# Moving two triangular systems and the sums of W_down inside an encoder layer on one core

## The chip, the core and the metric

The kernel runs as one program on 1 core of a Trainium2 chip. The metric is the device time of one execution in microseconds (us). A core has five engines: TensorE (PE; its weight loads are listed apart as PEld), VectorE (DVE), ScalarE (ACT), GpSimd (POOL) and SyncE (SP). SP computes nothing here; its queue issues most of the DMAs, in the order of the queue. Large weights are loaded through ACT's queue from the RWKV part on.

## What is computed

One layer (DEPTH = 1) over 1024 tokens of width 1024, all in float32:

```python
h = rmsnorm(x, g_mix[i])
z = h @ w_in[i]                       # FoX q, k, v, f | RWKV r, k, v, dw, da, dg | two gates
...
y_fox = fox_attention(q, k, v, log_f) # 8 heads of 64, causal, blocks of 128 queries
...
yr = rwkv7_scan(rh, decay, kh, vh, -kk, kk * ah)   # 8 heads of 64, a delta rule
y_rwkv = (yr + bonus) * g
merged = gate_fox * (y_fox @ w_o_fox[i]) + gate_rwkv * (y_rwkv @ w_o_rwkv[i])
x = x + merged @ w_out[i]
h2 = rmsnorm(x, g_ffn[i])
u = causal_dwconv(h2 @ w_up[i], conv_w[i], conv_b[i])
x = x + (gelu(u[..., :D_FF]) * u[..., D_FF:]) @ w_down[i]
ple_gate = sigmoid(rmsnorm(x, g_ple[i]) @ w_ple_gate[i])
x = x + ple_gate * (p[i] @ w_ple_up[i])
```

## The kernel before

**Arithmetic.** A float32 product is made of three matmuls: each operand is split into a high part (a cast on ACT) and the remainder (a subtraction, `L208`, on DVE), and high times high, low times high and high times low are added up in PSUM (`L236` to `L238` for most projections, `L734` and `L739` to `L741` for those of attention). The wide stage behind attention (FFN, `L1156`, `L1332`) is not touched.

**Stages in the order of the program.** Norm of x and the narrow projections; four calls of `rwkv_pre`, one per pair of RWKV heads (call 1 is `hp = 0`, call 4 is `hp = 3`); `fox_z(0)`, the projection of attention's first head pair, and `forget`, the forget gates; four pairs of attention (`fox_att`), each beside the projection of the next pair; then the RWKV chunk chain, gates, W_out, FFN.

**A call of `rwkv_pre`.** Projection of k (`L236` to `L238`); small products `L361` and `L369`; cumulative decay `L377`; norms of k: PE `L387`, DVE's root, ACT's copy `L394`, PE's transposes `L401`, DVE `L402` (`kkn`); projection of r; DVE `L407` to `L409` (`AR`), `L419` to `L423` (`kkn`, `kr`, `bk`), `L426` (`rk`); projection of v; `L433` (gate); transposes of v, `L442`; `L451` and DVE `L452`; then two groups of eight chunks: scores `L465` on PE, masked by DVE into `sc` (`L468`), stored by SP (`L474` to `L480`), transposes `L485` on PE, copied by ACT into `bt` (`L486`) and stored (`L488` to `L490`). SP also stores `AR` (`L412` to `L414`), the gate (`L435`), the transposed v (`L445`, `L446`) and `bvd` (`L453`).

**A triangular system, `tsolve(hp)`.** It needs the stored `sc` of call `hp + 1`. SP loads `tA` (`L513`, four DMAs), the generator yields `tlag`, POOL makes two copies into `tT` (`L517`), DVE does thirty steps of a product and an addition (`L521`, `L523`) and two memsets (`L527`): 62 DVE instructions in one chain, then SP stores and ACT copies the result (`L529` to `L532`). `tmerge` (`L548` to `L567`) makes the full inverse from it later, on PE.

**A sum of W_down, `down_sums`.** Eleven of them. SP loads two rows of blocks into `wt`, the only buffer (`L1258`), POOL makes four subtractions (`L1260` to `L1263`), SP stores four results (`L1266`), which the FFN reads.

**What sets the order.** Every stage is a generator that yields the cost of what it has issued, and `interleave` takes the generator that has done the least share of its stated cost:

```python
it = min(live, key=lambda e: e[2] / e[1])
it[2] += next(it[0]) or 0.0
```

The framework then orders each engine's instructions anew by its own estimate of when inputs will be there, so an operation can stand far from the place where the text issues it. Within an engine and a queue, that order is kept at run time.

In the kernel before, systems 1 to 3 (`tsolve(0)` to `tsolve(2)`) are beside calls 2 to 4, with `tlag` 30; system 4 (`tsolve(3)`) is beside `fox_z(0)`, with `tlag` 12; gate block 0 (`gate_early(0)`, whose matmuls read `gwh` and `gwl`) is beside call 4, block 1 beside `forget`; the sums are beside attention of pairs 1 to 3; the merges of systems 1 and 2 are beside pair 2, those of 3 and 4 beside pair 3.

Of the kernel before, what the change touches and what calls it, by code (L numbers as in the profile page):

```python
# [12 lines left out]
F32 = mybir.dt.float32  # L13
# [7 lines left out]
P = 128  # L21
# [6 lines left out]
HP = 4  # L28
DFF = 2816
NFB = DFF // P  # L30
# [22 lines left out]
def flat(gens):  # L53
    for g in gens:
        yield from g
# [7 lines left out]
def interleave(*parts):  # L63


    live = [[g, n, 0.0] for g, n in parts]
    while live:
        it = min(live, key=lambda e: e[2] / e[1])
        try:
            it[2] += next(it[0]) or 0.0  # L70
        except StopIteration:
            live.remove(it)


def merge(*gens):

    live = list(gens)
    while live:
        for g in list(live):
            try:  # L80
                yield next(g)
            except StopIteration:
                live.remove(g)


class Net:
# [1350 lines left out]
    def body(self, stop):  # L1437
# [63 lines left out]
        self.early = 7  # L1501
        self.cw = 160.0
        self.lora_w()
        self.p1, close_p1 = self.pool("rw", side="right")
        self.tlag = 30.0
        for hp in range(HP):
            side = [(self.tsolve(hp - 1), 40.0)] if hp else []
            if hp == HP - 1:
                side.append((self.gate_early(0, True, 35.0), 45.4))
            interleave((self.rwkv_pre(hp), 36.2), *side)  # L1510
        close_ps()
        close_ps = self.pools(("zp", 2), ("scp", 2), ("trp", 3), ("pvp", 1))
        close_p1()
        close_p0()
        close_wp()

        self.fwp, close_fwp = self.pool("foxw", side="right")
        self.fp, close_fp = self.pool("fox", side="right")
        self.kl = None
        zV, qk = [], []  # L1520
        self.tlag = 12.0
        self.wt, close_wt = self.pool("wt", side="left")
        self.wd2 = {n: self.tc.dram_tile([NFB // 2, P, 512], F32, name="wd" + n) for n in ("t1", "t2", "t3", "t4")}

        z_tile = lambda: self.zp.tile([P, 512], F32, name="z", tag="z")
        interleave((self.fox_z(0, self.fox_w(0), zV), 31.5), (self.tsolve(HP - 1), 22.0))
        interleave((flat([[3.0], merge(self.forget(), self.fox_qk(zV[0], qk))]), 5.7), (self.gate_early(1), 10.4))
        for hp in range(HP):
            att = self.fox_att(hp, qk, zV[1])
            if hp + 1 < HP:  # L1530
                zV, qk = [], []
                interleave((att, 23.0), (self.fox_z(hp + 1, self.fox_w(hp + 1), zV), 31.5),
                           (self.down_sums(range(hp * 4, min(hp * 4 + 4, NFB // 2))), 12.0),
                           *([(flat([self.tmerge(2 * hp - 2, z_tile), self.tmerge(2 * hp - 1, z_tile)]), 24.0)] if hp else []))
                interleave((merge(self.last, flat([[0.0] * 3, self.fox_qk(zV[0], qk)])), 6.0), (self.gate_early(hp + 2), 10.4))
            else:
                n = HP + 1

                def rest():
                    yield from att  # L1540
                    yield from self.last
                interleave((rest(), 25.0), (flat([self.gate_early(j) for j in range(n, self.early)]),
                                            10.4 * (self.early - n)))
        close_ps()
        close_fp()
        close_fwp()
        close_wt()
        close_gwp()
        close_tp()

# [80 lines left out]
        z_tile = lambda: self.zt.tile([P, T], F32, name="zt", tag="zt")  # L1631
# [182 lines left out]
```

## Time and profile before

| what | value |
|---|---|
| median of 3 runs | 1861.44 us (1861.11 to 1862.19) |
| profiled execution, its own time | 1862.91 us |
| its span in the trace | 1860.8 us |
| its mean granted PE clock | 0.988 of full speed |

The profile is of one execution, and its times are those of that execution. A row of the busy times gives an engine's busy time and its count of instructions. PE's matmuls are pipelined, and their ends are modelled. A row of the waits says which engine and line waited, for the instruction of which engine, how long in all, how many times, and the longest. Idle time of an engine on which nothing depends costs nothing.

### The profile page before, as it was taken

What the parts mean: (1) busy time and instruction counts of PE and PEld (TensorE: products, weight loads), DVE (VectorE), ACT (ScalarE), POOL (GpSimd) and SP (SyncE); (2) the same over time, 40 slices, a digit from 0 to 9 for tenths busy, and PEclk for the clock granted to TensorE, in tenths of its full rate; (3) what the DMA queues carried; (4) which work ended last, traced back from release to release, by engine and by line L of the source; (5) the groups of instructions that cost most, each with busy time, mean ns of one, the idle gap of its engine ahead of it and who ended that gap; (6) DMA issues with size and microseconds to landing.
All of it is one profiled execution on the core that took longest, in us unless ns stands there. A gap on an engine that the chain in (4) does not pass through costs nothing.

```text
span 1860.8 us, 28297 instructions
## 1 busy us (share of the span) xinstructions
PE 1789.9 (96%) x10867; PEld 1481.8 (80%) x10867; DVE 1207.4 (65%) x2382; ACT 783.0 (42%) x1236; POOL 357.9 (19%) x251
## 2 busy tenths in 40 slices
PE   5999998899999999999999999999999999999999
PEld 5876777788989776666778987888888888888898
DVE  7538655766565735545435288999899986566752
ACT  4543342457575622223362144344343444434431
POOL 4321001331000000000013304554545531000000
PEclk9999998899999999999999999999999999999999
DMA  6666548453122255545375123333233328655431
GB/s 200 196 195 193 133 92 220 139 158 97 32 75 55 69 137 125 163 134 142 122 245 161 57 91 85 119 107 103 85 97 118 107 95 317 234 198 176 144 117 46
DMA packets 295085, 250.29 MB, mean 135 GB/s; under 512 B 80200, under 2 KB 235550, under 8 KB 294951
## 3 DMA queue, kind: packets, MB, share of 16 engines
q1 hardware_dynamic: 230071, 220.40, 37.5%
q10 hardware_dynamic: 64880, 28.09, 6.0%
q8 instruction: 86, 1.41, 0.3%
q14 instruction: 48, 0.39, 0.1%
HBM read 171.07 MB, written 77.37 MB: 134 GB/s over the span
## 4 chain that ended last, share of the span: by engine, by line
PE 64%; DVE 3%; ACT 2%; DMA 1%; issue 1%; POOL 0%; ACTq 0%; DVEq 0%; POOLq 0%
PE pu L1156 8%; PE pu L1157 8%; PE pu L1158 8%; PE pu L1334 3%; PE pu L1333 3%; PE pu L1332 3%; PE zt L228 3%; PE zt L227 3%; PE zt L229 3%; PE zt L238 2%; PE zt L236 2%; PE zt L237 2%; PE zt L989 2%; PE zt L988 2%; PE zt L987 2%; PE tr L844 1%
## 5 line engine op out<-in xcount | busy, mean ns | idle before, releaser
L1332 PE MATMUL pu<-op 128*128 128x512 f32 x276 | 107.7, 390 | 0.0
L1334 PE MATMUL pu<-op 128*128 128x512 f32 x276 | 107.4, 389 | 0.0
L1333 PE MATMUL pu<-op 128*128 128x512 f32 x276 | 107.4, 389 | 0.0
L207 ACT CAST wh<-wr 128x1024 fp32r<-128x1024 f32 (+1 forms) x43 | 38.1, 889 | 142.4 <-PE zt L237 104.7
L236 PE MATMUL zt<-hah,wh 128*128 128x512 f32 (+1 forms) x200 | 79.4, 398 | 0.0
L237 PE MATMUL zt<-hbl,wh 128*128 128x512 f32 (+1 forms) x200 | 78.3, 391 | 0.0
L238 PE MATMUL zt<-hbh,wl 128*128 128x512 f32 (+1 forms) x200 | 78.1, 391 | 0.0
L236 PE MATMUL zt<-hbh,wh 128*128 128x512 f32 (+1 forms) x200 | 78.1, 391 | 0.0
L238 PE MATMUL zt<-hah,wl 128*128 128x512 f32 (+1 forms) x200 | 77.7, 389 | 0.0
L237 PE MATMUL zt<-hal,wh 128*128 128x512 f32 (+1 forms) x200 | 76.8, 384 | 0.0
L1166 DVE SCALAR_TENSOR_TENSOR u<-c,par,u 128x1023 f32<-128x1023 f32 x44 | 73.5, 1673 | 3.4 <-ACT u L1165 3.4
L208 DVE TENSOR_TENSOR op<-vh,op 128x1024 fp32r<-128x1024 f32 x38 | 45.4, 1222 | 46.3 <-ACT op L207 46.2
L1165 ACT ACTIVATE u<-c,par 128x1024 f32<-128x1024 f32 x44 | 54.6, 1243 | 49.0 <-DVE c L1242 38.4
L1167 DVE SCALAR_TENSOR_TENSOR u<-c,par,u 128x1022 f32<-128x1022 f32 x44 | 73.5, 1672 | 0.7
L1156 PE MATMUL pu<-hah,wh 128*128 128x512 f32 x176 | 70.3, 399 | 0.2 <-ACT hah L286 0.2
L1156 PE MATMUL pu<-t,vr 128*128 128x512 f32 x176 | 69.5, 395 | 0.5 <-DVE t L1074 0.5
L1157 PE MATMUL pu<-hal,wh 128*128 128x512 f32 x176 | 69.8, 397 | 0.0
L1158 PE MATMUL pu<-hah,wl 128*128 128x512 f32 x176 | 69.7, 396 | 0.0
L1157 PE MATMUL pu<-t,vr 128*128 128x512 f32 x176 | 69.4, 394 | 0.0
L1158 PE MATMUL pu<-t,vr 128*128 128x512 f32 x176 | 69.4, 394 | 0.0
L1157 PE MATMUL pu<-vl,vh 128*128 128x512 f32 x176 | 69.2, 393 | 0.0
L1156 PE MATMUL pu<-vh 128*128 128x512 f32 x176 | 69.0, 392 | 0.0
(534 smaller groups left out, 5588.2 us busy)
## 6 DMA issues: line engine op xcount, KB each, us to landing
X<-Xd SPq DMA_DIRECT2D x28, 448.0 KB
wt<-in_w_down SPq DMA_DIRECT2D x22, 512.0 KB
wdt<-wt SPq DMA_DIRECT2D x44, 256.0 KB
wr<-in_w_up SPq DMA_DIRECT2D x22, 512.0 KB
rr<-in_w_up SPq DMA_DIRECT2D x22, 512.0 KB
wr<-in_w_in ACTq DMA_DIRECT2D x21, 512.0 KB
mda<-u SPq DMA_DIRECT2D x33, 256.0 KB
mds<-sm SPq DMA_DIRECT2D x33, 256.0 KB
```

Source lines behind the costliest of these rows:

```text
L227: nc.tensor.matmul(ps, lhsT=lh, rhs=rh, start=(i == 0), stop=False)
L236: nc.tensor.matmul(o, lhsT=H[:, k, :], rhs=hh[:, k, :], start=(k == 0), stop=False)
L237: nc.tensor.matmul(o, lhsT=H[:, k, :], rhs=hl[:, k, :], start=False, stop=False)
L238: nc.tensor.matmul(o, lhsT=L[:, k, :], rhs=hh[:, k, :], start=False, stop=(k == NKB - 1))
L1156: nc.tensor.matmul(ps, lhsT=wh[:, k, :], rhs=bh[:, k, :], start=k == 0, stop=False)
L1157: nc.tensor.matmul(ps, lhsT=wh[:, k, :], rhs=bl[:, k, :], start=False, stop=False)
L1158: nc.tensor.matmul(ps, lhsT=wl[:, k, :], rhs=bh[:, k, :], start=False, stop=k == 3)
L1166: nc.vector.scalar_tensor_tensor(u[:, 1:T], c[:, 0:T - 1], cw(1), u[:, 1:T], op0=ALU.mult, op1=ALU.add)
L1167: nc.vector.scalar_tensor_tensor(u[:, 2:T], c[:, 0:T - 2], cw(0), u[:, 2:T], op0=ALU.mult, op1=ALU.add)
L1332: nc.tensor.matmul(ps[tb], lhsT=AH[:, j, ts], rhs=BH[:, j], start=f, stop=False)
L1333: nc.tensor.matmul(ps[tb], lhsT=AH[:, j, ts], rhs=BL[:, j], start=False, stop=False)
L1334: nc.tensor.matmul(ps[tb], lhsT=AL[:, j, ts], rhs=BH[:, j], start=False, stop=l)
```

## The change

Text only moves: no operation is added, removed or resized. Systems 1 and 2 stay beside calls 2 and 3. System 3 goes from call 4 to `fox_z(0)`, with `tlag` 4 instead of 12; system 4 goes from `fox_z(0)` to the end of the second pair's attention, behind the merges of systems 1 and 2. The eleven sums go from attention to calls 1 to 3 (four, four and three), and so the pool `wt` is opened and closed earlier.

```diff
--- before.py
+++ after.py
@@ -1501,37 +1501,41 @@
         self.early = 7
         self.cw = 160.0
         self.lora_w()
+        self.wt, close_wt = self.pool("wt", side="left")
+        self.wd2 = {n: self.tc.dram_tile([NFB // 2, P, 512], F32, name="wd" + n) for n in ("t1", "t2", "t3", "t4")}
         self.p1, close_p1 = self.pool("rw", side="right")
         self.tlag = 30.0
         for hp in range(HP):
-            side = [(self.tsolve(hp - 1), 40.0)] if hp else []
-            if hp == HP - 1:
-                side.append((self.gate_early(0, True, 35.0), 45.4))
+            if hp < HP - 1:
+                side = [(self.tsolve(hp - 1), 40.0)] if hp else []
+            else:
+                side = [(self.gate_early(0, True, 35.0), 45.4)]
+            if hp < HP - 1:
+                side.append((self.down_sums(range(hp * 4, min(hp * 4 + 4, NFB // 2))), 12.0))
             interleave((self.rwkv_pre(hp), 36.2), *side)
         close_ps()
         close_ps = self.pools(("zp", 2), ("scp", 2), ("trp", 3), ("pvp", 1))
         close_p1()
         close_p0()
         close_wp()
+        close_wt()
 
         self.fwp, close_fwp = self.pool("foxw", side="right")
         self.fp, close_fp = self.pool("fox", side="right")
         self.kl = None
         zV, qk = [], []
-        self.tlag = 12.0
-        self.wt, close_wt = self.pool("wt", side="left")
-        self.wd2 = {n: self.tc.dram_tile([NFB // 2, P, 512], F32, name="wd" + n) for n in ("t1", "t2", "t3", "t4")}
+        self.tlag = 4.0
 
         z_tile = lambda: self.zp.tile([P, 512], F32, name="z", tag="z")
-        interleave((self.fox_z(0, self.fox_w(0), zV), 31.5), (self.tsolve(HP - 1), 22.0))
+        interleave((self.fox_z(0, self.fox_w(0), zV), 31.5), (self.tsolve(HP - 2), 22.0))
         interleave((flat([[3.0], merge(self.forget(), self.fox_qk(zV[0], qk))]), 5.7), (self.gate_early(1), 10.4))
         for hp in range(HP):
             att = self.fox_att(hp, qk, zV[1])
             if hp + 1 < HP:
                 zV, qk = [], []
                 interleave((att, 23.0), (self.fox_z(hp + 1, self.fox_w(hp + 1), zV), 31.5),
-                           (self.down_sums(range(hp * 4, min(hp * 4 + 4, NFB // 2))), 12.0),
-                           *([(flat([self.tmerge(2 * hp - 2, z_tile), self.tmerge(2 * hp - 1, z_tile)]), 24.0)] if hp else []))
+                           *([(flat([self.tmerge(2 * hp - 2, z_tile), self.tmerge(2 * hp - 1, z_tile)] +
+                                    [self.tsolve(HP - 1)] * (hp == 1)), 24.0 + 17.0 * (hp == 1))] if hp else []))
                 interleave((merge(self.last, flat([[0.0] * 3, self.fox_qk(zV[0], qk)])), 6.0), (self.gate_early(hp + 2), 10.4))
             else:
                 n = HP + 1
@@ -1544,7 +1548,6 @@
         close_ps()
         close_fp()
         close_fwp()
-        close_wt()
         close_gwp()
         close_tp()
```

On SP, in call 3 (`hp = 2`, `Xd_618`), the difference reads as follows; `Ad_621` is what system 2 loads, and `wdt` are the stores of a sum.

```order
 L513 DMA tA<-Ad_621 32x32x32 x4
+L1258 DMA wt<-in_w_down 128x1024 x2
 L412 DMA Xd_618<-AR 64x1024
+L1266 DMA wdt_657<-wt 128x512
+L1266 DMA wdt_659<-wt 128x512
+L1266 DMA wdt_658<-wt 128x512
+L1266 DMA wdt_660<-wt 128x512
 L413 DMA Xd_618<-AR 64x1024
 L414 DMA Xd_618<-AR 128x1024
+L1258 DMA wt<-in_w_down 128x1024 x2
 L435 DMA gd_642<-tmp 128x1024
+L1266 DMA wdt_657<-wt 128x512
```

Three sums with their loads and stores now stand between the stores of `AR`, of the gate and of v in call 3; the call had none.

On PE, the end of call 4: first as it was, from the cumulative decay on (the rows go on with 25 more matmuls of the same projection before `L401`, then 73 of r and v before `L433`).

```order
L377 MATMUL ps<-tri,lw 128x128 x8
L387 MATMUL ps<-ind_91,tmp 128x2 x8
L237 MATMUL zt<-hal,wh 128x512
L238 MATMUL zt<-hah,wl 128x512
L236 MATMUL zt<-hah,wh 128x512
```

And as the change has it, from `L361` of the same call (`gwh` and `gwl` belong to gate block 0).

```order
L361 MATMUL ps<-zda,wa 128x512 x2
L236 MATMUL zt<-hbh,gwh 128x512
L237 MATMUL zt<-hbl,gwh 128x512
L238 MATMUL zt<-hbh,gwl 128x512
L369 MATMUL ps<-wd,dwT 128x128 x8
L377 MATMUL ps<-tri,lw 128x128 x8
L387 MATMUL ps<-ind_91,tmp 128x2 x8
L401 MATMUL ps<-ident,tmp 128x128 x8
L433 MATMUL ps<-sdg,wg 128x512 x2
L442 MATMUL ps<-ident,v 128x128 x8
L451 MATMUL ps<-tmp,bones 128x512 x2
L465 MATMUL ps<-AR,bk 128x128 x16
```

Behind the first rows no matmul of a projection is left in the call: those of k, r and v of call 4 and most of gate block 0 are now issued ahead of the last `L485` of call 3, 162 matmuls in all between `L465` and `L485` there.

On DVE, a piece near the end of the second pair's attention, as the change has it; `L850` is attention's split of the probabilities, `L785` and `L795` make the operands q and k of the next pair.

```order
L521 TENSOR_TENSOR tt<-tA,tT 128x110
L249 TENSOR_TENSOR ss<-ss,st_4041 128x16
L523 TENSOR_TENSOR tT<-tT,tt 128x10x11
L521 TENSOR_TENSOR tt<-tA,tT 128x110
L850 TENSOR_TENSOR pl<-tr,ph 128x384
L523 TENSOR_TENSOR tT<-tT,tt 128x11x10
L785 SCALAR_TENSOR_TENSOR q_5080<-sc,qn_114,q_5080 64x512
L521 TENSOR_TENSOR tt<-tA,tT 128x99
L795 SCALAR_TENSOR_TENSOR kl_3027<-sc,par,k_5082 64x512
L523 TENSOR_TENSOR tT<-tT,tt 128x11x9
L785 SCALAR_TENSOR_TENSOR q_5081<-sc,qn_114,q_5081 64x512
```

The steps of system 4 (`L521`, `L523`) stand singly between attention's instructions here, over some 125 rows of DVE from the third block of scores of the second head on; before, none of the systems was in this stretch.

## Rows read from the trace of the kernel before

**Rows 1.** The page: busy time, share of the span and instructions of each engine.

```profile
PE 1789.9 (96%) x10867; PEld 1481.8 (80%) x10867; DVE 1207.4 (65%) x2382; ACT 783.0 (42%) x1236; POOL 357.9 (19%) x251
```

**Rows 2.** Busy times by stretch: PE, PEld, DVE, ACT, POOL; clock, DMA share, GB/s.

```profile
116.00:300.50 184.50, 169.97 (x924) 131.63 (x922) 119.74 (x275) 74.49 (x98) 13.17 (x14) 0.97 0.58 151
337.00:376.00 39.00, 29.78 (x138) 24.87 (x137) 32.66 (x82) 22.52 (x39) 16.64 (x10) 0.83 0.60 171
376.00:433.00 57.00, 53.38 (x333) 47.41 (x333) 34.58 (x124) 31.09 (x75) 16.02 (x12) 0.97 0.46 146
503.00:535.40 32.40, 32.23 (x251) 27.78 (x249) 20.06 (x48) 24.23 (x44) 4.31 (x2) 1.00 0.23 62
```

**Rows 3.** Waits of PE, 116 to 300.5 us: total us, times, longest.

```profile
PE ps L485 <- DVE sc L468: 9.3, 5, 4.5
PE ps L465 <- DVE v L452: 2.6, 3, 1.1
PE z L734 <- ACT bt L486: 1.3, 1, 1.3
```

**Rows 4.** Waits of PE, 300.5 to 433 us.

```profile
PE z L918 <- DVE ft L910: 5.7, 1, 5.7
PE z L739 <- ACT sq L751: 2.6, 1, 2.6
PE sc L814 <- DVE st L819: 2.1, 1, 2.1
PE pv L861 <- DVE yf L870: 1.2, 1, 1.2
```

**Rows 5.** Busy times on tile tT alone: DVE, ACT, POOL; clock, DMA share, GB/s.

```profile
120.00:180.00 60.00, 18.27 (x62) 2.16 (x2) 1.22 (x2) 0.94 0.62 172
180.00:240.00 60.00, 15.01 (x62) 0.26 (x1) 1.22 (x2) 1.00 0.53 130
```

**Rows 6.** Timeline of POOL: start, us, instruction, idle before and its releaser.

```profile
155.91 1.77 POOL L1260 TENSOR_TENSOR wt<-wt 128x512 f32<-128x512 f32 x1 [25.72 <-DMA wt<-in_w_down]
157.76 1.27 POOL L1261 TENSOR_TENSOR wt<-wt 128x512 f32<-128x512 f32 x1
...
323.50 1.91 POOL L760 TENSOR_TENSOR z<-z,ss 128x1024 f32<-128x1024 f32 x1 [22.27 <-DVE ss L249]
325.35 1.28 POOL L517 COPY tT<-tA 64x512 f32<-64x512 f32 x2
```

**Rows 7.** Timeline of SP, 151 to 166 us.

```profile
151.02 0.81 SPq L1258 DMA_DIRECT2D wt<-in_w_down  x2
...
165.03 0.46 SPq L474 DMA_DIRECT2D Ad<-sc  x1
```

**Rows 8.** Timeline of PE, 164 to 192 us.

```profile
165.05 2.06 PE L465 MATMUL ps<-AR,bk 64*128 64x128 f32 x32
174.70 0.69 PE L485 MATMUL ps<-ident,bk 128*128 128x128 f32 x4 [2.03 <-DVE sc L468]
...
189.19 1.84 PE L387 MATMUL ps<-ind,tmp 128*128 128x2 f32 x16
```

**Rows 9.** Timeline of DVE: beside sums of POOL, and without.

```profile
91.35 2.30 DVE L426 SCALAR_TENSOR_TENSOR tmp<-r,par,kr 128x1024 f32<-128x1024 f32 x1
...
156.48 1.33 DVE L523 TENSOR_TENSOR tT<-tT,tt 128x110 f32<-128x110 f32 x1
...
169.53 0.27 DVE L523 TENSOR_TENSOR tT<-tT,tt 128x110 f32<-128x110 f32 x1
...
198.85 1.41 DVE L402 SCALAR_TENSOR_TENSOR kkn<-kr,par,ps 128x512 f32<-128x512 f32 x2 [4.28 <-PE ps L401]
...
208.37 1.28 DVE L426 SCALAR_TENSOR_TENSOR tmp<-r,par,kr 128x1024 f32<-128x1024 f32 x1
```

**Rows 10.** Timeline of ACT, 194 to 196 us.

```profile
194.60 1.05 ACT L394 COPY tmp<-rn 128x1024 f32<-128x1024 f32 x1 [1.16 <-DVE rn L249]
```

**Rows 11.** Waits of ACT, 55 to 300 us: total us, times, longest.

```profile
ACT fwh L207 <- DMA fwr<-in_w_in: 6.0, 2, 4.4
```

## Prediction

> **What bounds the kernel.** TensorE (PE) is busy 96% of the span [rows 1]. The change adds and removes no PE work, so time can come only from PE's waits and from its granted clock, in the stretch that is reordered. I read next the busy times by stretch [rows 2]: from 116 to 300.5 us (calls 2 to 4 of `rwkv_pre`, and gate block 0) PE works 170.0 of 184.5 us at a granted clock of 0.97; from 337 to 376 (end of the first attention projections, forget gates) 29.8 of 39 at 0.83; from 376 to 433 (first pair's attention) 53.4 of 57; from 503 to 535.4 (end of the second pair) 32.2 of 32.4. So the places to win are the first three; the fourth has nothing to win and something to lose.
>
> Then who ends the waits. In the RWKV calls it is VectorE (DVE) alone but for one: 9.3 us for the masked scores `sc` before the transposes of L485, 2.6 us for `v`, then 1.3 us at the end for ScalarE's copy `bt` [rows 3]. After that: 5.7 us for the forget gates `ft`, 2.6 us for the squares of a projection, 2.1 and 1.2 us in the first pair's attention [rows 4]. The largest of each list stands where a triangular system runs on DVE: systems 1 to 3 beside calls 2 to 4, the fourth beside the first projections. One system is 62 DVE instructions, 15.0 us busy where nothing disturbs it and 18.3 us where a sum of W_down runs on GpSimd (POOL) at the same time [rows 5].
>
> **What the sums do.** The program text has all eleven beside attention; in the built order six already stand before the RWKV calls end, and a sum's first subtraction starts at 155.9 us [rows 6]. So the change moves five sums. Each has two loads, four subtractions of about 1.3 us and four stores on SP's queue, which starts nothing out of order. From load to first subtraction 151.02 + 0.81 to 155.91 is 4.1 us [rows 6, 7]; the four take 1.77 + 3 x 1.27 = 5.6 us [rows 6]. So a sum whose stores come next on SP holds that queue for about 10 us, and the next load also waits for those stores to land.
>
> **Call 2 (about -1 us).** Two more sums now stand between its `vt` and `sc` stores. Before, the first store of `sc` left at 165.0 us [rows 7]. Now the sixth and seventh sums' transfers stand ahead of it; from the first `vt` store on, 10 us of hold, the landing and a second load put it near 172 us. The second group of `sc` reuses the buffers and starts 5 to 7 us later on DVE. PE has cover: 72 projection matmuls stand before L485 instead of 23. The 23 ran from 165.05 + 2.06 to 174.70 - 2.03, that is 167.1 to 172.7 us [rows 8], 0.24 us each, so 49 more are 11.8 us. The wait of 2.0 us goes. But the sixth sum's subtractions now run beside the first group of `sc`, between which seven small DVE instructions of system 1 stand; one such took 1.33 us beside POOL instead of 0.27 [rows 9], so up to 7 x 1.06 = 7 us, and 0 if they miss each other; most POOL time falls after the scores, and I take 2.4. With half of the slow-clock tail after the old wait, about -1.
>
> **Call 3 (about 0).** Its waits of `sc` (9.3 less 2.0 and 4.5 in calls 2 and 4: 2.8) go, since system 2 now stands behind the scores on DVE. But three sums run here, where none ran. The first falls on DVE's run from `kkn` to `rk`, eleven instructions from 198.85 to 209.65 us [rows 9], and the order now leaves only 35 projection matmuls (8.4 us) between L401 and the transposes of `v`, which stand behind that run. Lowest price: 0, if POOL waits. Highest: 4 x 1.3 = 5.2 us. The row of a long DVE instruction beside POOL, L426 with 2.30 us instead of 1.28 [rows 9], shows 1.0 us for one meeting; three meetings are 3 us. Taken: +3, net 0. The Trainium skill, page "SBUF — State Buffer", section "SBUF: two separate sides", says that a VectorE instruction with two SBUF inputs and a GpSimd instruction that reads SBUF lock each other out for whole instructions; with every subtraction winning once that is the upper end, and would add 2 us to the sum. The rows show the lock, but also POOL losing (1.77 us for 1.3).
>
> **Call 4 (+7.5).** This is the bill. System 3 leaves DVE here, and with it the 4.5 us wait, 1.3 for `bt` and about 1.5 of small ones, mostly `v` [rows 3]: -7.3. But the order now issues all projections of call 4 and most of gate block 0 before call 3's last L485, so behind L361 only 3 matmuls of any projection are left, and call 4's elementwise chain lies open. From rows of call 3: L387 ends at 191.03, the copy that L401 reads ends at 195.65 [rows 8, 10]: 4.6 us. From L402 to the end of L426 10.8 us, less one long instruction (1.28) for `r`, which now comes earlier: 9.5, of which L401 and L442 (sixteen transposes; four of L485 take 0.7 to 1.05 [rows 8]) and the two of L433 cover about 3: 6.5 us. Two `v` products, two splits (long instructions like those of rows 9, partly met) and the first `sc` before PE may transpose: 2 to 3. Added 14, net +6.7, and +0.8 because the next projection starts on a clock that such gaps have lowered. Low end +2 (DVE and ACT quicker with no system running), high end +16 (second rival).
>
> **First projections and forget gates (-9).** System 4 could start only at 325.35 us: its two copies on POOL stood behind L760, which waited 22 us for DVE [rows 6], and ended beside the forget chain. System 3 has its input since call 3; its copies now stand ahead of L760 and its DVE work is spread over the projection. The waits of 5.7 and 2.6 us [rows 4] are 8.3 of the 9.2 us in which PE was idle there (29.8 of 39 us busy), and the low clock (0.83 of 39 us [rows 2]: 6.6 us) goes in part with them: 13 us at most. But ACT now copies the solved system inside the forget chain, and the chain itself is not shorter, so I take two thirds: -9, ends -4 and -13.
>
> **First pair's attention (-3.5).** Three sums and the last of system 4 leave it: 2.1 + 1.2 us of waits and up to 2 of clock. Ends 0 and -5.5.
>
> **Second pair (+5).** System 4 now runs beside its last 32 us. DVE is busy 20.1 of 32.4 us there [rows 2] and has 12.3 us left; the system wants 15.0 to 18.3. Overflow 2.7 to 6, and the q/k operands of the next pair are last in that line. Ends 0 (PE's own work covers a late DVE) and +8. From the middle of the third pair on, every engine's order is the same as before.
>
> **Sum.** -1 + 0 + 7.5 - 9 - 3.5 + 5 = -1. Against the profiled execution, 1862.91 us by its own time (span 1860.8), that is 1861.9; the median of the runs shown is 1.5 us lower, so **1860.4**. About 0.2% (3.7 us) is what a measurement of this kernel can tell from no change.
>
> **Rivals.** *The gains come without the bills*: POOL and DVE miss each other, ACT and DVE run call 4's chain quicker once no system stands in it, the system fits into DVE's gaps. -3 + 0 + 3 - 11 - 4 + 3 = -12, less if one fails: about 1851. For it: call 1 has four sums beside it already and DVE had gaps there. Against: the call-4 chain is short of matmuls whatever DVE does.
> *Slower*: in call 4 the copies of `bt` stand on ACT behind the casts of the first attention weights, and these behind their loads; ACT waited 6.0 us for two such loads before [rows 11], hidden by matmuls and by DVE's lateness. With the chain bare, two loads of up to 4.4 us are added to it: 14 + 9 instead of 14, sum +8 to +10, about 1870.5. It decides if the second of these loads is issued later than the end of L426: then `bt`, L465 and the last L485 wait for it one after another.
> *The change does less than it says*: the sums that mattered were already early, and the two systems only trade places, each costing PE in its new place what it cost in the old. 1861.
>
> **Chances.** Forecast 0.40 (own range 1855 to 1866: 0.09 faster by over 0.2%, 0.26 within, 0.05 slower), gains alone 0.24, slower 0.26, trade of places 0.10 (within). Together 0.33 faster, 0.36 within 0.2%, 0.31 slower. The range reaches from the first rival's time to just past the second's: 1851 to 1871.
>
> **What would show it.** Right: PE's wait for `ft` under 3 us and no wait for `sc` of 4.5 us; PE's busy share between L361 and L465 of call 4 near 60%; system 4's DVE instructions between scores of the second pair, with new PE waits there of 3 to 8 us; the projection of the first pair starting 4 to 8 us later than 300.5. Wrong: a start at or before 300 us, no new waits in the second pair, or waits in call 3 of over 6 us, which would mean that SP's queue and not DVE sets it.

## The result and the profile after

The changed kernel took 1884.57 us in the median of 5 runs (1878.58 to 1888.04), the kernel before 1861.11 (1857.59 to 1862.19, 5 runs): a ratio of 1.0126, interval 1.0105 to 1.0147. It is some 23 us slower, and outside the range of 1851 to 1871. The profiled execution took 1888.04 us, the longest of the five, with a span of 1886.3.

PE's busy time on the page, beside 1789.9 us before [rows 1]:

```profile
PE 1795.8 (95%) x10867; PEld 1485.3 (79%) x10867; DVE 1224.4 (65%) x2382; ACT 785.2 (42%) x1238; POOL 362.5 (19%) x251
```

The same work keeps PE busy 6 us longer; the other 20 us by which the span grew are idle time of PE. Where, the starts of some of PE's instructions in the timelines tell (us; `L361` is near the start of a call, the first `L734` ends the RWKV calls, `L918` is the forget gates' matmul, the first `L782` of a pair makes its q and k, `L622` starts the chunk chain). In the program's order of all kernels here 546 matmuls stand before the `L361` of call 2, and 1260 before the first `L734`:

| | L361, call 2 | first L734 | L918 | L782, pair 2 | L782, pair 3 | L782, pair 4 | L622 |
|---|---|---|---|---|---|---|---|
| before | 120.4 | 300.5 | 352.0 | 438.0 | 522.0 | 607.1 | 680.7 |
| the change | 123.6 | 325.6 | 378.1 | 452.7 | 538.3 | 632.2 | 705.8 |

So calls 2 to 4 take 21.9 us longer (202.0 instead of 180.1), the stretch from there to `L918` loses 0.9, from `L918` to the second pair's operands 11.4 are gained, and from there to the fourth pair's operands 10.5 are lost. The 3.2 us ahead of call 2 are at the same order of PE. The kernels below start call 2 at 116.7 to 118.3, but for the two with transfers on POOL's queue (126.9 and 124.3); what that stretch owes is left out of the account, and where a start is called so much "ahead of before", 2 to 4 us of it were there at call 2.

Busy times by stretch, of the change: calls 2 to 4, the forget gates, the first pair's later part, and the end of the second pair (columns as in [rows 2]).

```profile
116.00:325.60 209.60, 176.77 (x925) 136.31 (x925) 129.64 (x229) 75.19 (x98) 42.53 (x31) 0.92 0.66 189
362.00:400.00 38.00, 30.51 (x163) 25.73 (x163) 24.56 (x71) 27.58 (x51) 5.07 (x2) 0.91 0.45 114
400.00:447.90 47.90, 46.72 (x313) 43.18 (x311) 32.00 (x109) 28.38 (x67) 1.91 (x1) 1.00 0.11 31
517.00:560.00 43.00, 38.36 (x223) 33.61 (x222) 40.54 (x124) 27.79 (x50) 5.36 (x2) 0.96 0.17 46
```

Before, DVE was busy 119.7 us in calls 2 to 4 [rows 2]; now it is 129.6 us with 46 instructions fewer, beside 42.5 us of POOL instead of 13.2, and the granted clock is 0.92 instead of 0.97. At the end of the second pair DVE is nearly full: 40.5 of 43 us.

PE's waits in calls 2 to 4 (116 to 325.6 us), which answer [rows 3]:

```profile
PE ps L485 <- DVE sc L468: 13.7, 5, 5.4
PE ps L451 <- DVE tmp L426: 7.1, 1, 7.1
PE ps L442 <- DVE v L305: 6.1, 2, 4.1
PE ps L401 <- ACT tmp L394: 4.7, 1, 4.7
PE ps L465 <- DVE sc L468: 1.8, 2, 1.5
PE z L734 <- ACT bt L486: 0.9, 1, 0.9
```

From there to 447.9 us, which answers [rows 4], and from 500 to 600 us:

```profile
PE z L918 <- DVE ft L910: 5.8, 1, 5.8
PE z L734 <- ACT fwh L207: 1.7, 1, 1.7
PE sc L814 <- DVE st L819: 1.2, 1, 1.2
...
PE sc L782 <- DVE q L785: 4.0, 1, 4.0
PE pv L861 <- DVE yf L870: 1.5, 2, 1.2
```

The bare call 4, the one without projections to fill PE's time, is there (`L401`, `L451`), with its 4.5 us wait for `sc` not gone but grown to 5.4; so are waits for `v`, of 4.1 us in call 2, which was not forecast, and of 2.0 in call 3; the wait for `ft` is the old one.

### The profile page after: what moved, and what is told of

Same layout as the page of the kernel before. It is cut to its first block, busy times and chain, and to the rows that moved or that the text cites. A ratio compares the mean times of both kernels' runs of the same rounds, so it can differ in the third digit from the quotient of the medians.

```text
span 1886.3 us, 28305 instructions
## 1 busy us (share of the span) xinstructions
PE 1795.8 (95%) x10867; PEld 1485.3 (79%) x10867; DVE 1224.4 (65%) x2382; ACT 785.2 (42%) x1238; POOL 362.5 (19%) x251
## 4 chain that ended last, share of the span: by engine, by line
PE 78%; DVE 11%; ACT 4%; DMA 4%; issue 2%; SPq 1%; POOL 0%; ACTq 0%; DVEq 0%; POOLq 0%
PE pu L1156 8%; PE pu L1157 8%; PE pu L1158 8%; PE zt L236 3%; PE pu L1334 3%; PE pu L1332 3%; PE pu L1333 3%; PE zt L238 3%; PE zt L237 3%; PE zt L228 3%; PE zt L229 3%; PE zt L227 3%; DVE tt L521 2%; DVE tT L523 2%; PE z L739 2%
## 5 line engine op out<-in xcount | busy, mean ns | idle before, releaser
L208 DVE TENSOR_TENSOR op<-vh,op 128x1024 fp32r<-128x1024 f32 x38 | 45.4, 1222 | 45.8 <-ACT op L207 45.7
```

## The experiments

**Which half of the change.** Three kernels: the sums alone, the systems alone, the fourth system alone. Edits of `sums_only` against the kernel before (the pool `wt` is opened ahead of the calls, as in the change):

```diff
+            else:
+                side.append((self.down_sums(range(hp * 4, min(hp * 4 + 4, NFB // 2))), 12.0))
...
-                           (self.down_sums(range(hp * 4, min(hp * 4 + 4, NFB // 2))), 12.0),
```

> The eleven sums go beside calls 1 to 3 as in the change; the four triangular systems stay where they were before. Theory 'sums' (the loss is made by the sums: they reorder PE, so that call 4 has no projection left, and hold DVE and SP in call 2): PE's first L734 starts 20 to 26 us later than before's 300.5, the run takes 1875 to 1886 us. Rival 'systems' (the loss comes from the moved systems, above all the fourth beside attention): L734 within 4 us of 300.5, 1856 to 1866 us.

Measured: 1883.58 us, ratio 1.0136 (1.0115 to 1.0156). The first `L734` starts at 329.5, the run is as slow as the whole change, and PE's order in the calls is that of the change. In its waits of calls 2 to 4 one row has grown:

```profile
PE ps L485 <- DVE sc L468: 20.4, 4, 16.3
```

With system 3 left in call 4 the bare call is worse still: 16.3 us before its last `L485`. All sixty steps of the system stand on DVE between the two groups of scores there (308.9 to 326.1 us).

`systems_only` has the other half of the diff (both `tsolve` lines and `tlag` 4; sums as before).

> Systems 3 and 4 go where the change has them; the sums stay beside attention. Theory 'sums': PE's order in the four calls is that of before, L734 starts at 296 to 301 us, the first pair's attention gains 7 to 11 us and the second pair loses 6 to 11, so 1852 to 1863 us. Rival 'systems': 1875 us or more, with the waits of call 4 (L401, L451) as in the change.

Measured: 1860.83 us, ratio 1.0016 (1.0005 to 1.0028). First `L734` at 296.1, `L782` of pair 2 at 425.8 (12.2 us ahead of before), of pair 4 at 605.2 (1.8 ahead): the systems gain 10 us up to the first pair's end and lose them by the fourth's operands. The text puts system 3 beside `fox_z(0)`, but the framework's order runs its steps at 274.8 to 303.3 us, beside call 4 as before; so this kernel tests the move of system 4, and not that of system 3. The bill of the second pair is the fourth system's, here as in the change (`L782` waits 4.0 us for q in both).

`fourth_only` leaves system 3 beside call 4:

```diff
-        interleave((self.fox_z(0, self.fox_w(0), zV), 31.5), (self.tsolve(HP - 1), 22.0))
+        interleave((self.fox_z(0, self.fox_w(0), zV), 31.5))
```

> Only system 4 moves to the end of the second pair; system 3 and the sums as before. If system 4 is what cost the forget gates 5.7 us and the first pair its waits: these go and the second pair's waits of the change come, 1856 to 1866 us, and the wait of 4.5 us for sc in call 4 stays. If the wait for ft is the gates' own chain (it is 5.8 us in the change too), it stays at 5 to 6 us here and the run is 1863 to 1871 us.

Measured: 1860.45 us, ratio 1.0009 (0.9996 to 1.0023), no difference that can be told. The wait for `ft` falls to 1.8 us when system 4 leaves, so it was not the gates' own chain. PE's waits of that kernel, 300 to 433 us:

```profile
PE sc L814 <- DVE st L819: 2.1, 1, 2.1
PE z L918 <- DVE ft L910: 1.8, 1, 1.8
```

So the loss of 23 us is the sums': five of them, since six stood beside the calls before. What in them?

**The wait for the scores.** Is the wait before the last `L485` a system on DVE, as the prediction had it, or the two buffers of `sc`? `sc4` is the kernel before with `bufs=4` for `sc`.

> The kernel before with four buffers for sc instead of two. Theory 'stores' (the second group of masked scores waits until the stores of the first group have landed, so the 4.5 us wait before the last L485 of call 4 has nothing to do with a system on DVE): PE's waits of L485 for sc (9.3 us in calls 2 to 4) fall under 3 us and the run gains 4 to 9 us, 1852 to 1857 us. Rival (as predicted: the system's instructions on DVE hold the scores up): the waits stay within 2 us of 9.3, 1859 to 1863 us.

Measured: 1868.4 us, ratio 1.0053 (1.0039 to 1.0068): slower, against the forecast, though the mechanism held. PE's wait of `L485` in calls 2 to 4 fell from 9.3 [rows 3] to 2.3 us and the first `L734` came at 292.1, 8.4 us earlier (3.6 of them at call 2 already):

```profile
PE z L734 <- ACT bt L486: 5.7, 1, 5.7
PE ps L485 <- DVE sc L468: 2.3, 4, 0.8
```

System 3 was still beside call 4 (258.9 to 293.5 us). But all eleven sums now start between 318.8 and 482.4 us, beside the forget gates and the first two pairs (in the kernel before six had started by 155.9 us, the first at 38.6). That is not what took the wait away: `late_sums` below has no sum beside the calls either, keeps two buffers, and its `L485` waits 9.0 us. Where the sums stand now, the kernel loses 14 us up to the third pair's operands. That the larger pool leaves no room for `wt` during the calls may be why they moved; it was not tried.

**The order, the lock or SP's queue.** Three things about the sums could cost: the order of PE that comes with them; a lock, by which a subtraction of POOL and an instruction of DVE with two inputs in SBUF wait for each other; or the transfers in SP's queue. `nosub` is the change without the four subtractions (W_down's sums become copies of its blocks). Its order of PE still leaves call 4 bare: 1151 matmuls stand ahead of its `L361` (1163 in the change, 1022 before).

```diff
-            gp.tensor_sub(w[:, 0, lo], w[:, 0, hi], w[:, 0, lo])
...
-            gp.tensor_sub(w[:, 1, lo], w[:, 1, lo], w[:, 1, hi])
```

> The change without the four subtractions of each sum (W_down's sums are then plain copies of its blocks). POOL does nothing for the sums; loads and stores stay in SP's queue, and PE's order still leaves call 4 without projections. Theory 'queue': call 4 keeps its waits (L401 about 4.7, L451 5 to 7, L485 about 5 us) and the first L734 comes 12 to 20 us later than before's 300.5; the run takes 1870 to 1882 us. Rival 'lock': these waits fall below half, first L734 within 6 us of 300.5, 1866 us or less.

Measured: 1860.68 us, ratio 1.0007 (0.9996 to 1.0019), between the two theories: call 4 keeps its wait for `L426`, and yet the run is as fast as before.

```profile
PE ps L451 <- DVE tmp L426: 7.8, 1, 7.8
PE ps L485 <- DVE sc L468: 5.0, 2, 4.4
PE ps L401 <- ACT tmp L394: 2.1, 1, 2.1
```

The 129 matmuls drawn ahead (31 us at 0.24) save in calls 2 and 3 what they cost in call 4: `L361` of call 4 starts 16.9 us later than before instead of 31.0, 14.1 ahead (11.0 without the head start at call 2), and 10.8 are given back by the first `L734`, at 297.1. So the bare call alone is no loss against the kernel before: calls 2 to 4 take 179.8 us instead of 180.1. `late_systems` below, with no sum beside the calls and projections in call 4, takes 176.9, so the order and the transfers cost at most some 3 us. `locksub` then adds the subtractions again, into a scratch buffer that nothing reads, with PE's order and the order of SP's transfers as in `nosub`:

```diff
+            x = self.wt.tile([P, 512], F32, name="wx", tag="wx", bufs=1)
+            gp.tensor_sub(x, w[:, 0, hi], w[:, 0, lo])
+            gp.tensor_sub(x, w[:, 1, hi], w[:, 0, hi])
+            gp.tensor_sub(x, w[:, 1, hi], w[:, 0, lo])
+            gp.tensor_sub(x, w[:, 1, lo], w[:, 1, hi])
```

> The change with each sum's four subtractions written into a scratch buffer, so that its stores (plain copies of the blocks of W_down) wait for the loads alone. PE's order and SP's queue are those of nosub, and POOL's 44 subtractions run beside calls 1 to 3 as in the change. Theory 'lock' (POOL's subtractions and DVE's instructions with two inputs in SBUF shut each other out, and the delay on DVE is the loss): most of the 24 us between nosub and the change come back, 1874 to 1886 us, and a system's own DVE time in call 2 is 22 to 26 us as in the change (25.7), not 15.1 as in nosub. Theory 'queue' (what costs is that stores stand in SP's queue behind sums that wait for POOL): 1858 to 1866 us, as nosub.

Measured: 1876.86 us, ratio 1.0095 (1.0068 to 1.0123). Busy times from 116 us to the first `L734`, of `nosub` and of `locksub`:

```profile
116.00:297.15 181.15, 163.64 (x908) 127.68 (x906) 105.23 (x225) 75.42 (x98) 6.75 (x8) 0.96 0.73 205
```

```profile
116.00:313.00 197.00, 170.51 (x910) 130.21 (x908) 126.03 (x225) 75.43 (x98) 41.30 (x31) 0.94 0.67 189
```

The same 225 instructions of DVE, in the same order, take 126.0 us instead of 105.2: 20.8 us, for 24 subtractions in that stretch. Some 15 of them are on the 120 steps of systems 1 and 2 (`L521`, `L523`), most of the rest on `L426`, `L208`, `L246` and `L248`. `L248`, which has a single input, was held once too (1.15 us instead of 0.17). The maskings `L468`, which read one input from PSUM, kept their 0.68 to 0.69 us even where a subtraction ran beside them. A system's own instructions show it too (tile tT, first the change, then `nosub`, then `locksub`; columns as in [rows 5]):

```profile
110.00:200.00 90.00, 25.74 (x62) 2.16 (x2) 1.21 (x2) 0.91 0.67 198
200.00:262.00 62.00, 22.35 (x56) 0.00 (x0) 1.82 (x2) 0.99 0.71 204
```

```profile
110.00:200.00 90.00, 15.07 (x62) 2.16 (x2) 2.67 (x4) 1.00 0.78 215
200.00:262.00 62.00, 15.10 (x62) 2.15 (x2) 0.00 (x0) 1.00 0.64 191
```

```profile
110.00:200.00 90.00, 22.83 (x62) 2.17 (x2) 1.21 (x2) 0.96 0.72 203
```

From the `L361` of call 2 to the first `L734` it is 179.8 us in `nosub`, 194.8 in `locksub` and 202.0 in the change (180.1 before). So 15.0 of the 22.2 us between `nosub` and the change, two thirds, are the meetings of POOL and DVE. In the last step the stores, in SP's queue, wait for the subtractions as well, and the order changes (12 more matmuls ahead of the `L361` of call 4, another order on SP); which of the two costs the other 7.2 us was not separated. In the whole time that step is 1.0095 to 1.0126, and the two intervals overlap, so its size is not firm. PE's wait for `v` (`L442`, 5.8 us in `locksub`) is there with the lock and absent from `nosub`'s list.

`q_gp` tries the other side: the whole change, with the sums' transfers on POOL's queue.

```diff
-                nc.sync.dma_start(w[:, j], self.a["w_down"][(j * H + i) * P:(j * H + i) * P + P, :])
+                nc.gpsimd.dma_start(w[:, j], self.a["w_down"][(j * H + i) * P:(j * H + i) * P + P, :])
...
-                nc.sync.dma_start(self.wd2[n][i], w[:, j // 2, j % 2 * 512:j % 2 * 512 + 512])
+                nc.gpsimd.dma_start(self.wd2[n][i], w[:, j // 2, j % 2 * 512:j % 2 * 512 + 512])
```

> The whole change, but the sums' loads and stores are issued from POOL's queue instead of SP's; the order of PE in the calls is then that of before but for a few projections, with eleven sums still beside the calls. Theory 'queue' (the sums cost what they do because their transfers stand in SP's queue ahead of the stores of sc, which the ordering sees too): no wait of L401 or L451 in call 4, first L734 at 290 to 302 us, and the run within 6 us of systems_only, 1853 to 1866 us. Rival 'lock' (POOL's subtractions hold DVE, whatever the queue): first L734 8 to 20 us later than before's 300.5 and 1870 us or more.

Measured: 1873.61 us, ratio 1.0079 (1.0059 to 1.0098). With SP's queue free and with as many matmuls ahead of each `L361` as before, calls 2 to 4 still take 192.8 us instead of 180.1, and nearly all of it is call 2: its `L361` to that of call 3 takes 74.0 us instead of 60.7. `L401` waits 0.3 us in all and `L451` is absent. The last sum begins at 197.2 us; call 3, behind it, takes 56.3 us instead of 55.9, and system 2 15.1 us of DVE. Another 6.5 us are lost ahead of call 2, which this account does not explain. A system's own DVE time in call 2 is nearly that of the change:

```profile
110.00:200.00 90.00, 24.88 (x62) 2.16 (x2) 1.55 (x2) 0.89 0.82 254
```

`b_gp` makes that edit alone, on the kernel before.

> The kernel before with one thing changed: the sums' loads and stores are issued from POOL's queue. With that the ordering puts all eleven sums beside the calls by itself, and the systems stay. Theory 'queue': the sums beside the calls are cheap then and leave the first pair's attention, which gains 2 to 5 us: 1852 to 1860 us. Rival 'lock': 1865 us or more.

Measured: 1870.51 us, ratio 1.0068 (1.0052 to 1.0084). With the loads off SP's queue the ordering by itself starts all eleven sums before 200 us, and the calls pay for it as in `q_gp`. A queue is no cure for the lock.

**A better place.** If POOL's subtractions cost where DVE is waited for, they belong where PE has no gaps: pairs 2 to 4. `late_sums` ties them there, by a copy that cannot run before the pair's q is made.

```diff
             w = self.wt.tile([P, 2, D], F32, name="wt", tag="wt", bufs=1)
+            gp.tensor_copy(w[:, 0:2, 0:1], tie)
...
+            tie = qk[0][0][:, 0:2].bitcast(F32).unsqueeze(2)
```

> The kernel before with no sum beside the calls: a copy of two columns from the pair's q into the sum's buffer ties four sums to the second pair's attention, four to the third's and three to the fourth's. Systems as before. Theory 'lock': calls 1 to 3 lose the meetings of POOL and DVE (the first L734 comes 4 to 12 us earlier than before's 300.5), the first pair gains 2 to 5 us, and pairs 2 to 4, where PE hardly waits, give back 0 to 6 us: 1842 to 1857 us. Rival (a sum costs the same wherever it stands): 1857 to 1866 us.

Measured: 1858.15 us, ratio 0.9992 (0.9976 to 1.0008): no difference, and in the range of the rival, that a sum costs the same wherever it stands. The first `L734` comes at 295.1 and `L782` of pair 2 at 422.8, 15.2 us ahead of before; 5 of these are gone at pair 3, 3 more at pair 4, and 7 in the fourth pair (`L622` at 680.3).

`late_systems` adds the change's places for systems 3 and 4 in the text; system 3's steps again run beside call 4 (272.7 to 300.5 us).

> late_sums with systems 3 and 4 where the change has them. The first pair gains what it did in systems_only (some 8 us against before at L782 of the second pair's operands), and the end of the second pair pays for system 4 (7 to 10 us) and now also for sums beside it: within 3 us of late_sums, or up to 8 us slower if sums and system 4 meet on DVE.

Measured: 1858.59 us, ratio 1.0001 (0.9983 to 1.0018). `L782` of pair 2 at 413.4, 24.6 us ahead of before, and of pair 4 at 600.0, 7.0 ahead: the stretch between, with sums and system 4, takes back nearly 18.

`pair1_four` therefore ties system 4 to the first pair, which no longer has sums (its steps run at 356.9 to 397.9 us, those of system 3 beside call 4); `pair1_sums65` also moves the fourth pair's sums forward (six in the second pair, five in the third).

```diff
+        if tie is not None:
+            nc.gpsimd.tensor_copy(tA[:, 0, 0:2], tie)
...
+                             else [(self.tsolve(HP - 1, tie[:, :, 0]), 22.0)]))
```

> late_systems with system 4 tied to the first pair's attention (by a copy of two columns of the pair's q into its buffer) instead of the end of the second pair; system 3 beside the first projections, no sum before the second pair. If system 4 costs at the end of the second pair because its steps stand on DVE ahead of the next pair's q and k, the 12 us that late_systems lost between L782 of the second and of the fourth pair's operands shrink to the 8 of late_sums, the first pair gives back 2 to 6 us, and the run takes 1848 to 1856 us. If a system costs 8 to 12 us in any pair of attention, 1856 to 1864 us.

> pair1_four with the sums six in the second and five in the third pair, none in the fourth, where late_sums lost 7 us for three sums. If that loss belongs to the fourth pair, 3 to 6 us better than pair1_four; if it only goes with the number of sums (about 1.3 us each), within 2 us of it.

Measured: 1853.79 us, ratio 0.9979 (0.9967 to 0.9991), and 1852.78 us, ratio 0.9971 (0.9959 to 0.9982), against 1857.33 for the kernel before in the same set. Both are 0.2 to 0.3% faster than the kernel before, a small gain but clear of the intervals, and far ahead of the change. In `pair1_four`, `L782` of pairs 2, 3 and 4 starts 23.5, 18.9 and 17.3 us ahead of before; 7 are lost by `L622` again. In `pair1_sums65` that loss is gone, but pairs 2 and 3 lose 13. The two end within their intervals of each other, and from the second pair's operands to `L622` both lose 13 us for eleven sums: by these two runs the price goes with the number of sums and not with the pair.

## Why the prediction was wrong

**Where the miss lies.** `L361` of call 4 starts 43.6 us later with 141 more matmuls done, which are 33.8 us at the prediction's 0.24; so 9.8 were lost by then, 3.2 ahead of call 2 and 6.5 inside calls 2 and 3. By the same reckoning call 2 has 43 and call 3 has 98 of these matmuls more. Call 2 then cost 6.4 us (forecast -1), call 3 0.2 (0) and call 4 15.3 (+7.5); the gates and the first pair together gave 10.5 (12.5), and the way to the fourth pair's operands cost 10.5 (+5). Rows by call show what the subtractions did, first of the change, then of `nosub` (columns as in [rows 2]):

```profile
123.62:200.96 77.34, 67.82 (x345) 52.26 (x344) 52.55 (x97) 28.59 (x35) 18.48 (x14) 0.93 0.62 188
200.96:280.56 79.60, 76.24 (x399) 59.83 (x398) 52.24 (x97) 27.02 (x34) 19.95 (x14) 1.00 0.64 183
280.56:325.60 45.04, 25.18 (x161) 18.30 (x160) 22.92 (x31) 19.46 (x29) 4.10 (x3) 0.79 0.74 197
```

```profile
117.35:176.92 59.57, 58.51 (x326) 46.20 (x325) 40.65 (x97) 27.64 (x33) 1.21 (x2) 1.00 0.78 232
176.92:253.87 76.95, 76.95 (x406) 61.26 (x405) 41.80 (x97) 27.13 (x34) 1.45 (x2) 1.00 0.66 187
253.87:297.15 43.28, 26.83 (x173) 19.43 (x172) 22.79 (x31) 19.57 (x29) 4.08 (x4) 0.84 0.76 201
```

Without subtractions PE works through calls 2 and 3 almost without a gap, and these gain 7.1 and 3.9 us by that reckoning, against 10.8 lost in call 4.

**Calls 2 and 3 (forecast -1 and 0, found 6.4 and 0.2).** The step that failed is the size of the lock in call 2: 2.4 us, with 7 as its upper end, from the seven small instructions of system 1 between the scores. The system's own DVE time there grew by 10.7 us (25.74 instead of 15.07), because POOL met its steps all along and not only those seven: the system does not only stand among the scores, it stands ahead of them. In call 3 the forecast held, and for its reasons: no wait for `sc` is left, and the run from `kkn` to `rk`, priced at 3, costs a wait for `v` of 2.0 us. System 2 took longer there too (22.4 us of DVE for 56 of its instructions), behind the first scores, while PE had 162 projections to do. POOL and DVE of the change in call 2:

```profile
183.63 1.29 POOL L1261 TENSOR_TENSOR wt<-wt 128x512 f32<-128x512 f32 x1 [0.73 <-DMA wt<-in_w_down]
184.99 1.29 POOL L1262 TENSOR_TENSOR wt<-wt 128x512 f32<-128x512 f32 x1
```

```profile
183.78 1.20 DVE L521 TENSOR_TENSOR tt<-tA,tT 128x42 f32<-128x42 f32 x1
185.01 1.33 DVE L523 TENSOR_TENSOR tT<-tT,tt 128x42 f32<-128x42 f32 x1
...
194.23 2.47 DVE L468 TENSOR_TENSOR sc<-ps,smask 128x512 f32<-128x512 f32 x4
```

```profile
188.60 2.19 ACT L531 COPY tX<-tT 32x512 f32<-32x512 f32 x2 [17.53 <-DVE tT L523]
190.81 1.05 ACT L207 CAST wh<-wr 128x1024 fp32r<-128x1024 f32 x1
```

Steps of 0.2 us (`L521` of these 42 elements took 0.20 before) wait out whole subtractions of 1.3 us; the system ends late, ACT stands behind it with `L531` and then casts the next weights, DVE splits those, and only then come the scores (194.2) for which PE waits 3.6 us in spite of 72 projections. The Trainium skill, page "SBUF — State Buffer", section "SBUF: two separate sides", gives the lock for the whole instruction to whichever starts first. The trace agrees: steps of DVE last up to as long as a whole subtraction, and POOL loses too, but less. The 24 subtractions of `locksub` cost DVE 20.8 us, 0.87 us each, while they took 33.6 us themselves, 1.40 us each instead of the shortest 1.26.

**Call 4 (+7.5 forecast, +15.3 found: 25.1 less 9.8).** The mechanism was right: the projections are gone and `L401` and `L451` wait, 11.8 us, near the 4.6 and 6.5 forecast; PE is busy 16.9 of the 28.7 us from `L361` to `L465`, the 60% that were forecast. The failed step is "System 3 leaves DVE here, and with it the 4.5 us wait". In the kernel before that wait was not the system's: it is 5.4 us in the change and 4.4 in `nosub`, where system 3 has left the call, and `sc4` ends it with the system still there. In the change DVE stands idle ahead of the scores, until stores have landed:

```profile
321.99 2.53 DVE L468 TENSOR_TENSOR sc<-ps,smask 128x512 f32<-128x512 f32 x4 [6.19 <-DMA Xd<-sc]
```

The second group reuses the two buffers of `sc`, and the last store of the first leaves SP at 318.8. Besides, one DVE instruction of the bare chain met a split on POOL (`L208`, 3.00 us):

```profile
300.17 3.00 POOL L208 TENSOR_TENSOR fwl<-gwr,fwh 128x1024 fp32r<-128x1024 f32 x1 [42.44 <-ACT fwh L207]
```

```profile
300.88 3.37 DVE L422 TENSOR_TENSOR bk<-kkn,iP 128x1024 f32<-128x1024 f32 x1
```

With these gaps the granted clock is 0.79 over call 4 (0.95 before), for which 0.8 us was put; no row of before shows that term, and no run separates what the clock cost here. And the price of the bare call was set against call 4 alone. `nosub` has it too and loses nothing against before, because calls 2 and 3 get the matmuls: the bill is real when those calls are held up by POOL.

**First projections and forget gates (-9 forecast, +0.9 found).** The step "its DVE work is spread over the projection" failed. System 3's loads leave SP only at 329.1 us; it has 56 of its instructions between 350 and 372 us in the change and ends beside the forget chain as system 4 did. Its last step meets a split on POOL (2.37 us instead of 0.17), and its copy on ACT and a table load (`L244`) that did not stand there before come ahead of the chain's own table load (`L908`):

```profile
371.14 2.14 ACT L531 COPY tX<-tT 32x512 f32<-32x512 f32 x2 [1.66 <-DVE tT L523]
373.30 1.28 ACT L244 ACT_TABLE_LOAD   x1
...
375.30 1.28 ACT L908 ACT_TABLE_LOAD   x1
```

The 5.8 us wait is the same wait with another system in it. Where no system stands in that place (`systems_only`, `fourth_only`, with system 3 beside call 4 and system 4 later), it is 1.8 us.

**First pair (-3.5 forecast, -11.4 found)** and **second pair (+5 forecast, +10.5 found).** Right in sign, both too small. But `L918` lies in the middle of the prediction's stretch from 337 to 376 us: by the count of matmuls, whose order differs there in part, the first stretch gave about 4.6 (low end 4) and the first pair about 5.8 (high end 5.5). Together the forecast had 12.5, and they gave 10.5. In the second pair the q and k operands were late as predicted (`L782` waits 4.0), and the rest is small waits and clock as the fourth system goes on into the third pair: `systems_only` loses 10.4 there without any sum. The 12.3 us of room on DVE [rows 2] did not keep the system inside the second pair: it took 18.67 us of DVE, just over the 18.3 forecast, but spread over the 38 us from 519.9 to 557.6.

**The rivals.** The slower one named the wrong mechanism: `bt` waited for its stores and for PE, not for weights, and PE's wait for `bt` is 0.9 us. "The sums that mattered were already early" was wrong outright: `sums_only` moves five sums and loses as much as the whole change.

## What to carry to other kernels

Before POOL work goes beside a stretch, count DVE's instructions with two inputs in SBUF there, small steps too, and charge DVE with some two thirds of POOL's busy time (20.8 of 33.6 us here); then ask which of DVE's results PE waits for. Price a reordering over all the stages that trade matmuls, not where the gap appears. And read the releaser of the waiting engine itself: the wait for `sc` was named after DVE, while DVE was waiting for a store. Last, look up where the framework has put what the text moves: in `systems_only`, `late_systems`, `q_gp` and both `pair1` kernels system 3 stayed beside call 4.

## What the runs showed that was not expected

The same small DVE chain, 62 instructions, took 15.1 us of DVE's time undisturbed and 22.8 to 25.7 us beside POOL, and these steps bore some 15 of DVE's 20.8 us in `locksub`. Four buffers for `sc` removed the wait they were meant to remove and made the kernel slower by 0.5%. Sums cost about 1.2 us each (13 for eleven) even in pairs 2 to 4, where PE had hardly waited.
